# Hybrid encoder layer on one core: two gate projections moved behind the delta rule's first front, and attention's half of the output projection cut into 32 column-half units placed along the delta rule

## The chip, the cores and the metric

The kernel runs on one core of a Trainium2 chip. A core has five engines with their own instruction queues: TensorE (PE, matmuls, with PEld for the loads of its stationary operand), VectorE (DVE), ScalarE (ACT), GpSimd (POOL) and SyncE (SP), which here issues every DMA. Engines wait for each other through semaphores; each takes its instructions in the order in which they were written into its queue. The metric is the device time of one execution in microseconds (us).

## What is computed

One layer over a sequence of 2048 rows of 1024 features, in fp32:

```python
h = rms_norm(x, norm_w)
proj = h @ w_in
dn_q, dn_k, dn_v, dn_z, dn_beta, dn_decay, sw_q, sw_k, sw_v, sw_z = jnp.split(proj, cuts, axis=-1)
dn = gated_deltanet_bidir(dn_q, dn_k, dn_v, dn_beta, dn_decay, ...)   # 4 heads of 128, conv of 5, chunks, both directions
dn = rms_norm(dn, dn_out_norm_w) * silu(dn_z)
sw = windowed_gqa_with_sinks(sw_q, sw_k, sw_v, ...) * silu(sw_z)      # 8 query heads of 64, |i-j| <= 128
x = x + concatenate([dn, sw]) @ w_out
```

The delta rule solves a unit triangular system per chunk (the inverse of I + M), and then carries a 128 x 128 state through the chunks, forward and backward.

## The kernel before, in words

The sequence is 16 chunks of 128 rows, in two halves of eight. `phase_a` does the projections, the convolutions and attention; `phase_b` the delta rule and the output projection. Products that need more than one fp32r pass are split into a high and a low part, and three fp32r matmuls of 512 columns (hi x hi, hi x lo, lo x hi) add up in PSUM (L186 to L188, L558 to L560). Matmuls of the delta rule are plain fp32, which the profile records as two matmuls each.

For each half, `phase_a` projects keys, values and queries (L197 to L199), and then runs attention chunk by chunk (`attend`, L327 on: scores L339/L340, maximum L341, exponential L346, scaling L355, transposes L360, split L364/L365, product with the values L367/L368). Between chunks it writes "fillers" into the program: `gate_pairs` (tiles `pf_z`, 96 matmuls each: two pairs for attention's gates zsw, two for the delta rule's gates zdn) and `conv_pair` (tiles `pf_c`, 96 matmuls each, six pairs, with five VectorE taps at L237). `nfill` (L381) says how many fillers follow each chunk; in the second half it took six of ten, and the other four were written behind attention.

`phase_b` works head by head (0 to 3). `pre_front(h)` loads keys and queries (`kq`), transposes them (`tr`, L641), forms the Gram products (`gh`, L661), scales them with decays into the matrices `ma` (L670), writes the part to be inverted to DRAM (`m_d`) and scales the values (`trv`, L678). `pre_back(h)` reads `m_d` back into L, solves 32 x 32 blocks by 31 dependent pairs of VectorE operations (`tm`, L707, and `X`, L711), writes them to `x_d`, reads them in other layouts (`xc`) and completes the inverse with fp32 matmuls (`pi`, L735) and copies on GpSimd and ScalarE. `scan(h)` runs 16 steps in two directions: state times key (`pk`, L775), the residual `r` (L777), `py` (L784), `yk` (L789), the new state (L793, L796) and the outputs (L786, L802, `oacc`). `post` normalises them and writes `mix_dn`. A scan loads its keys and queries (`kqc`, L773) into four buffers per direction. In the program `pre_front(h + 1)` and `pre_back(h + 1)` follow `scan(h)`; the matrices of heads h and h + 2 share buffers (`hd[h % 2]`).

`out_sw` (L564) is attention's half of the output projection: it takes the attention results `mix_sw` chunk by chunk, splits them (`mhs` L550, `mls` L551), multiplies them with four row blocks of `w_out` (`wohs` L542, `wols` L543) into two PSUM tiles of 512 columns (`pcs`), adds the residual x (`xrs`, L561) and writes the sum to `part` in DRAM. It stands in the program between head 0's front and its solve, and its weights stay in SBUF for all 16 chunks. `out_dn` adds the delta rule's half (`pcd`) to `part` at the end. `warm` (L847) is 32, 32 and 20 matmuls of the identity with itself behind heads 1, 2 and 3; nothing reads them.

The order on each engine isn't that of the program. `set_order` (L892) takes all instructions with their dependences, the rings of buffers and the pools that share memory (a pool's users wait for those of the pool that held the space), gives each a price from `cost` and a delay from `LAG`, plans the five queues against each other, backward and forward, twelve times, and writes the order of the best plan into the program as fixed. It runs before the kernel is built; on the chip each engine follows that order.

Line numbers are those of the kernel before.

Of the kernel before, what the change touches and what calls it, by code (L numbers as in the profile page):

```python
# [7 lines left out]
F32 = mybir.dt.float32  # L8
F32R = mybir.dt.float32r
# [15 lines left out]
NDEC = 1  # L25
NEG = -1e30


def tile_hybrid(ctx, tc, t, out, dbg=None):
# [26 lines left out]
    with ExitStack() as ca:  # L56
        consts = phase_a(ca, tc, t, ident, nw, bd, gp, mix_sw, kq_d, v_d, zdn_d, zsw_d, dp)
    with ExitStack() as cb:
        phase_b(cb, tc, t, ident, consts, hp, mix_dn, mix_sw, kq_d, v_d, zdn_d, zsw_d, dp, out)
# [4 lines left out]
def phase_a(ctx, tc, t, ident, nw, bd, gp, mix_sw, kq_d, v_d, zdn_d, zsw_d, q_pool):  # L64
# [5 lines left out]
    with tc.using_default_side("right"):  # L70
        xp = ctx.enter_context(tc.tile_pool(reuse_waits="tile", name="xp", bufs=2))
        wp = ctx.enter_context(tc.tile_pool(reuse_waits="tile", name="wp", bufs=2))
        bp = ctx.enter_context(tc.tile_pool(reuse_waits="tile", name="bp", bufs=5))
        pj = ctx.enter_context(tc.tile_pool(reuse_waits="tile", name="pj", bufs=3, space=PSUM))
# [306 lines left out]
    nfill = ((2, 1, 1, 1, 1, 1, 1, 2), (2, 1, 1, 1, 1, 0, 0, 0))  # L381
# [40 lines left out]
    with tc.high_priority(-1000000):  # L422
        for f in fill:
            f()
    return consts
# [91 lines left out]
def phase_b(ctx, tc, t, ident, consts, hp, mix_dn, mix_sw, kq_d, v_d, zdn_d, zsw_d, dp, out):  # L517
# [57 lines left out]
    with tc.using_default_side("right"):  # L575
        hd = [pool("hd0"), None]
        q1 = pool("q1")
        ps_i = [pool("ps_i0", stack=pre_stack, space=PSUM)]
        ps_t = pool("ps_t", stack=pre_stack, space=PSUM)
        ps_g = pool("ps_g", stack=pre_stack, space=PSUM)  # L580
    rp = pool("rp", 2)
    qp = pool("qp", stack=pre_stack)
    ps_s = pool("ps_s", space=PSUM)
    ps_i.append(pool("ps_i1", stack=pre_stack, space=PSUM))
    XE = V
    zts = [[const(f"iv{j}_{i}", [P, 4, P], None, qp) for i in range(2 - j % 2)] for j in range(4)]
    for grp in zts:
        for a in grp:
            G.memset(a, 0.0)
# [10 lines left out]
    def kv_tile(kind, h, n, name):  # L600
        p, slot = ((0, n), (1, n), (2, n) if n < 2 else (0, n - 2), (0, 2 + n) if n < 2 else (1, n - 2))[h]
        return (hd[p] if p < 2 else qp).tile([P, 4, P], F32, tag=f"{kind}{slot}", name=name, bufs=1)

    def pre_front(h):
# [12 lines left out]
        for n, c4 in enumerate(FRONT):  # L617
# [71 lines left out]
    def pre_back(h, H):  # L689
        ma = H["ma"]  # L690
        m_d, x_d, mp = H["solve"]
        L0 = qp.tile([64, 32, 32], F32, tag="L0", name=f"L0{h}")
        L = qp.tile([P, 32, 32], F32, tag="L", name=f"L{h}")
        X = qp.tile([P, 32, 32], F32, tag="X", name=f"X{h}")
# [5 lines left out]
        G.memset(x, 0.0)  # L700
# [536 lines left out]
```

## Time and profile before

| | us |
|---|---|
| time, median of 3 runs | 1336.02 (1333.45 to 1339.87) |
| span of the profiled execution, first to last instruction | 1337.1 |
| PE / DVE / ACT / POOL busy in it | 1265.9 / 886.6 / 707.6 / 487.9 |
| mean granted TensorE clock | 0.988 |
| bytes moved by DMA | 199.10 MB, mean 149 GB/s |

The profile is of one execution; its span is the only time that it gives for that execution, and it lies within the spread of the runs. "Busy" is the time in which at least one instruction of the engine is recorded; records of successive matmuls overlap, so that a busy share near 100% doesn't yet mean that matmuls start as close as they can. The last column of a group of instructions is the idle time ahead of it and who ended it. A window row gives the busy time of each engine between two times, with the number of instructions in brackets.

### The profile page before, as it was taken

Reading aid. Unit: us, or ns where it says so; the run is one execution under the profiler, and the core shown is the slowest. Engines: PE = TensorE matmul, PEld = TensorE weight load, DVE = VectorE, ACT = ScalarE, POOL = GpSimd, SP = SyncE. Lnnn points to the kernel's source line nnn. Section 1 sums busy time; section 2 is a strip of 40 time slices with the busy share of each in tenths; the row PEclk is TensorE's granted clock in tenths of the full one; section 3 lists DMA queues with packets and bytes.
Section 4 is the critical chain, followed back from the end, with each engine's and each line's share of the span. In section 5 each row is a group of like instructions: output and inputs, shape, how many; then the busy total and the mean of one; then the engine's idle time right before and its main releaser. Section 6 shows DMA issues by size and latency. Waiting matters only on the chain.

```text
span 1337.1 us, 22922 instructions
## 1 busy us (share of the span) xinstructions
PE 1265.9 (95%) x7330; PEld 1083.1 (81%) x7330; DVE 886.6 (66%) x2250; ACT 707.6 (53%) x2105; POOL 487.9 (36%) x876
## 2 busy tenths in 40 slices
PE   5999999999999999999999899999979989898998
PEld 4998878888789988888888678778869878798776
DVE  4413387999856324778987898567884987846433
ACT  5422254766544333334766866229757867566310
POOL 1223033575602321002677654328238247070000
PEclk8999999999999999999999999999999999999999
DMA  7442344222552444323222767968476364333776
GB/s 243 129 139 82 115 142 133 98 88 93 177 178 88 134 146 135 114 71 105 87 94 93 264 198 228 279 197 214 121 193 171 97 198 117 97 107 107 230 239 216
DMA packets 219113, 199.10 MB, mean 149 GB/s; under 512 B 48240, under 2 KB 170736, under 8 KB 218992
## 3 DMA queue, kind: packets, MB, share of 16 engines
q1 hardware_dynamic: 218992, 197.63, 48.5%
q8 instruction: 59, 0.97, 0.3%
q14 instruction: 62, 0.51, 0.1%
HBM read 132.50 MB, written 65.08 MB: 148 GB/s over the span
## 4 chain that ended last, share of the span: by engine, by line
PE 67%; DVE 10%; DMA 9%; ACT 6%; POOL 3%; issue 2%; SPq 1%; DVEq 0%; POOLq 0%; ACTq 0%
PE pf_c L186 6%; PE pf_c L187 6%; PE pf_c L188 5%; PE pf_z L186 4%; PE pf_z L187 4%; PE pf_z L188 4%; PE pi L735 3%; PE pt L360 3%; PE pq_q L197 2%; PE pq_q L198 2%; PE pq_q L199 2%; PE pcd L559 2%; PE pcd L560 2%; PE pcd L558 2%; DMA xc<-x_d 2%
## 5 line engine op out<-in xcount | busy, mean ns | idle before, releaser
L237 DVE SCALAR_TENSOR_TENSOR acc<-pf_c,cw,acc 128x512 f32<-128x512 f32 (+1 forms) x192 | 140.1, 743 | 30.4 <-ACT acc L233 27.0
L186 PE MATMUL pf_c<-xhi,wh_c 128*128 128x512 f32 x384 | 148.7, 399 | 1.7 <-DVE acc L237 1.6
L187 PE MATMUL pf_c<-xlo,wh_c 128*128 128x512 f32 x384 | 148.5, 399 | 0.0
L188 PE MATMUL pf_c<-xhi,wl_c 128*128 128x512 f32 x384 | 147.7, 397 | 0.0
L355 POOL TENSOR_SCALAR pr<-pr,st 128x384 f32<-128x384 f32 (+1 forms) x128 | 84.4, 678 | 83.5 <-DVE st L353 59.1
L188 PE MATMUL pf_z<-xhi,wl_z 128*128 128x512 f32 x256 | 94.3, 400 | 0.0
L186 PE MATMUL pf_z<-xhi,wh_z 128*128 128x512 f32 x256 | 94.1, 399 | 0.0
L187 PE MATMUL pf_z<-xlo,wh_z 128*128 128x512 f32 x256 | 93.6, 397 | 0.0
L346 ACT ACTIVATE pr<-pr,st 128x384 f32<-128x384 f32 (+1 forms) x128 | 76.0, 596 | 27.1 <-DVE st L345 24.2
L186 PEld LDWEIGHTS pf_c<-xhi,wh_c 128*128 128x128 f32 x384 | 72.1, 188 | 17.6 <-DVE acc L237 2.2
L188 PEld LDWEIGHTS pf_c<-xhi,wl_c 128*128 128x128 f32 x384 | 72.1, 188 | 15.2
L187 PEld LDWEIGHTS pf_c<-xlo,wh_c 128*128 128x128 f32 x384 | 72.1, 188 | 14.3
L364 ACT ACTIVATE ph<-pt 128x512 fp32r<-128x512 f32 x92 | 53.7, 595 | 50.1 <-PE pt L360 42.4
L341 DVE CUSTOM_DVE_ANT_0 pr<-s,mask,sink 128x384 f32<-128x384 f32 (+1 forms) x128 | 72.9, 591 | 8.4 <-PE s L340 5.7
L360 PE MATMUL pt<-ident,pr 128*128 128x128 f32 x368 | 70.8, 276 | 2.5 <-POOL pr L355 2.1
L365 DVE TENSOR_TENSOR pl<-pt,ph 128x512 fp32r<-128x512 f32 x92 | 62.0, 683 | 12.7 <-ACT ph L364 11.6
L789 ACT ACTIVATE yk<-py,ck 128x128 f32<-128x128 f32 x120 | 44.1, 367 | 43.6 <-PE py L784 40.9
L360 PEld LDWEIGHTS pt<-ident,pr 128*128 128x128 f32 x368 | 47.8, 141 | 19.0 <-POOL pr L355 5.9
L670 DVE SCALAR_TENSOR_TENSOR ma<-gh,bp,dc 128x256 f32<-128x256 f32 x128 | 56.0, 475 | 10.2 <-PE gh L661 8.1
L233 ACT ACTIVATE acc<-pf_c,cw 128x512 f32<-128x512 f32 x48 | 32.6, 682 | 54.3 <-PE pf_c L188 48.8
L197 PE MATMUL pq_q<-wh_q,xhi 128*128 128x256 f32 x256 | 58.5, 284 | 0.2 <-ACT sgq L256 0.2
L561 DVE TENSOR_TENSOR xrd<-xrd,pcd 128x512 f32<-128x512 f32 x32 | 20.9, 683 | 55.8 <-PE pcd L560 48.0
(254 smaller groups left out, 3795.2 us busy)
## 6 DMA issues: line engine op xcount, KB each, us to landing
kqc<-kq_d SPq DMA_DIRECT2D x120, 128.0 KB, 2.6
ws_c<-wt SPq DMA_DIRECT2D x48, 256.0 KB, 3.6
xr<-x SPq DMA_DIRECT2D x16, 512.0 KB, 5.7
ws_z<-wt SPq DMA_DIRECT2D x32, 256.0 KB, 3.5
kq<-kq_d SPq DMA_DIRECT2D x16, 512.0 KB, 4.9
xrs<-x SPq DMA_DIRECT2D x32, 256.0 KB, 3.9
part<-xrs SPq DMA_DIRECT2D x32, 256.0 KB, 3.4
m_d<-ma SPq DMA_DIRECT2D x32, 256.0 KB, 4.8
```

Of the source, the lines that this page charges most:

```text
L186: T.matmul(ps, hi[:, k, cs], xhi[b][:, k], start=(k == 0), stop=False)
L187: T.matmul(ps, hi[:, k, cs], xlo[b][:, k], start=False, stop=False)
L188: T.matmul(ps, lo[:, k, cs], xhi[b][:, k], start=False, stop=(k == KC - 1))
L197: T.matmul(ps[:, :n], xh, hi[:, k, :n], start=(k == 0), stop=False)
L237: V.scalar_tensor_tensor(av, ps[:, lo:], cw[:, i, k : k + 1], av, ALU.mult, ALU.add)
L341: V.tensor_tensor_reduce(pr[j][:, :n], ps[:, :n], mask[:, lo * P : hi * P], 1.0, sink[:, hh : hh + 1], ALU.add, ALU.max, accum_out=mx[:, j ...
L346: A.activation(pr[j][:, :n], pr[j][:, :n], AF.Exp, bias=nm[:, j : j + 1], accum_out=den[:, j : j + 1])
L355: G.tensor_scalar(pr[j][:, :n], pr[j][:, :n], den[:, j : j + 1], 1.0, ALU.mult, ALU.mult)
L360: T.transpose(pt[:, j], pr[j][:, (kb - lo) * P : (kb - lo + 1) * P], ident)
L364: A.activation(ph, ptf, AF.Copy)
L365: V.tensor_tensor(pl, ptf, ph.bitcast(F32), ALU.subtract)
L670: V.scalar_tensor_tensor(ma[d, c4][:, c], gh[:, k], bp[:, d, cc : cc + 1], gms[d][:, c : c + 1].to_broadcast([P, 2, P]), ALU.mult, ALU.mult,)
```

## The change

- `nfill` of the second half becomes (2, 1, 1, 1, 1, 1, 1, 0): all six convolution pairs lie between chunks of attention. The remaining two fillers, the gate pairs of zdn, are handed to `phase_b` as `late` and written behind `pre_front(0)`. The pools that projections need (`xp`, `wp`, `bp`, `pj`) stay open until then, in a stack of their own (`wide`).
- `pre_back` is cut into `solve` (the 31 pairs) and `invert`. L0 is gone: the first half of L lands in X, is copied transposed out of it, and X is cleared afterwards. Pools are regrouped: `qa` for the solve, `qb` for the inversion.
- `out_sw` becomes `sw_units`: 32 units of one chunk and one half of the columns. A unit loads and splits its chunk itself, so that each chunk is loaded and split twice; the weights are loaded by halves of the columns into one set of buffers. Eight units are written ahead of `invert(0)`, one behind each group of the fronts of heads 2 and 3 (`FILLF`), and the last 16 behind `invert(3)`; PSUM is taken from tiles of the fronts and the inversion in turn.
- `warm` is gone.
- The planner's prices of five kinds of instruction change, and it gets more SBUF: the program's scratch for dynamic DMA shrinks from 16 KB to 1 KB per partition.

```diff
+N0 = 8
+FILLF = ((0, 0, 0, 0), (1, 1, 1, 1), (1, 1, 1, 1))
...
-    nfill = ((2, 1, 1, 1, 1, 1, 1, 2), (2, 1, 1, 1, 1, 0, 0, 0))
+    nfill = ((2, 1, 1, 1, 1, 1, 1, 2), (2, 1, 1, 1, 1, 1, 1, 0))
...
-    with tc.high_priority(-1000000):
-        for f in fill:
-            f()
-    return consts
+    return consts, fill
...
-    def out_sw(pool, bank, order):
-        w = load_wo(pool, 4, "s", "s")
-        for n, c in enumerate(order):
-            sc = slice(c * P, (c + 1) * P)
-            mx = pool.tile([P, 4, P], F32, tag="mx", name=f"mxs{c}", bufs=2)
+    def sw_units(pool):
+        w = {}
+
+        def weights(j):
+            wh = pool.tile([P, 4, 512], F32R, tag="wohs", name=f"wohs{j}", bufs=1)
+            wl = pool.tile([P, 4, 512], F32R, tag="wols", name=f"wols{j}", bufs=1)
+            for k in range(4):
+                st = pool.tile([P, 512], F32, tag="ws", name=f"woss{j}_{k}")
+                dma(st, t["wout"][:, 4 + k, j * 512 : (j + 1) * 512])
+                A.activation(wh[:, k], st, AF.Copy)
+                V.tensor_tensor(wl[:, k], st, wh[:, k].bitcast(F32), ALU.subtract)
+            w[j] = wh, wl
+
+        def unit(c, j, bank):
+            if j not in w:
+                weights(j)
+            wh, wl = w[j]
+            ns = slice(j * 512, (j + 1) * 512)
+            mx = pool.tile([P, 4, P], F32, tag="mx", name=f"mxs{c}_{j}", bufs=SWB[0])
             dma(mx, mix_sw[c])
-            out_half(pool, lambda j, nm: bank(n, j, nm), w, mx, t["x"][sc, :], part_d[c], f"s{c}", MB)
+            mh = pool.tile([P, 4, P], F32R, tag="mh", name=f"mhs{c}_{j}", bufs=SWB[1])
+            ml = pool.tile([P, 4, P], F32R, tag="ml", name=f"mls{c}_{j}", bufs=SWB[1])
+            A.activation(mh, mx, AF.Copy)
+            V.tensor_tensor(ml, mx, mh.bitcast(F32), ALU.subtract)
+            xr = pool.tile([P, 512], F32, tag="ws", name=f"xrs{c}_{j}")
+            dma(xr, t["x"][c * P : (c + 1) * P, ns])
+            ps = bank(f"pcs{c}_{j}")
+            for k in range(4):
+                T.matmul(ps, mh[:, k], wh[:, k], start=(k == 0), stop=False)
+                T.matmul(ps, ml[:, k], wh[:, k], start=False, stop=False)
+                T.matmul(ps, mh[:, k], wl[:, k], start=False, stop=(k == 3))
+            V.tensor_tensor(xr, xr, ps, ALU.add)
+            dma(part_d[c][:, ns], xr)
+
+        todo = [(c, j) for j in range(2) for c in range(NCH)]
...
+            if h:
+                for k in range(FILLF[h - 1][n]):
+                    fill(1, bank(k % 2))
...
-        dma(L0, lv[0])
+        dma(X[0:64], lv[0])
         dma(L[64:128], lv[1])
         x = X.rearrange("p r c -> p (r c)")
+        V.tensor_copy(L[0:64], X[0:64].rearrange("p r c -> p c r"))
         G.memset(x, 0.0)
         G.memset(x[:, ::33], 1.0)
-        V.tensor_copy(L[0:64], L0.rearrange("p r c -> p c r"))
...
-    def warm(h):
-        idle = ps_s.tile([P, P], F32, tag="pk", name=f"warm{h}")
-        for _ in range((32, 32, 20)[h]):
-            T.matmul(idle, ident, ident, start=True, stop=True)
+    def bank(k):
+        return lambda nm: (ps_t, ps_g, ps_i[0], ps_i[1])[k].tile([P, 512], F32, tag=("tr", "gh", "inv", "inv")[k], name=nm)
 
     H = pre_front(0)
+    for f in late:
+        f()
+    solve(0, H)
+    wide.close()
...
-    pre_back(0, H)
+    fill = sw_units(swp)
+    for n in range(N0):
+        fill(1, bank(2 + n % 2))
+    invert(0, H)
     for h in range(3):
         scan(h, H)
         H = pre_front(h + 1)
-        pre_back(h + 1, H)
-        warm(h)
+        solve(h + 1, H)
+        invert(h + 1, H)
+    for k in range(32):
+        fill(1, bank(k % 2))
...
             if "float32r" in str(i.ins[0].dtype):
-                return max(112, m / 2.4 + 14)
+                return max(112, 0.441 * m + 4)
...
-            return 60 + 0.86 * m + 85 * (scalars > 0) + 110 * (len(o) > 1)
+            short = len(o[0].ap) > 2 and o[0].ap[-1][1] <= 64
+            return 60 + 0.86 * m + 85 * (scalars > 0) + 110 * (len(o) > 1) + 100 * short
...
-        return 150 + 1.02 * m
+        return 190 + 1.02 * m
...
+        if eng[k] == "PE" and not insts[k][0].is_transpose and "float32r" not in str(insts[k][0].ins[0].dtype):
+            lag += 40
```

More of the change, by code (lines that the diff above doesn't have):

```diff
@@ L54, in tile_hybrid, with phase_a @@
     mix_dn = dp.tile([4, P, S], F32, tag="mix_dn", name="mix_dn")
[L56 to L59, printed above, removed]
+    with ExitStack() as cb, ExitStack() as wide:
+        with ExitStack() as ca:
+            consts, late = phase_a(ca, wide, tc, t, ident, nw, bd, gp, mix_sw, kq_d, v_d, zdn_d, zsw_d, dp)
+        phase_b(cb, wide, late, tc, t, ident, consts, hp, mix_dn, mix_sw, kq_d, v_d, zdn_d, zsw_d, dp, out)
     if dbg is not None:
         dbg(tc, locals())
[L64 removed]
+def phase_a(ctx, wide, tc, t, ident, nw, bd, gp, mix_sw, kq_d, v_d, zdn_d, zsw_d, q_pool):
     nc = tc.nc
@@ L514, in delta_setup, with phase_b @@
     return dmask, dnw, pw, beta, negc, ngc, egt, ekd, egc, gr_d, dec_d
-def phase_b(ctx, tc, t, ident, consts, hp, mix_dn, mix_sw, kq_d, v_d, zdn_d, zsw_d, dp, out):
+def phase_b(ctx, wide, late, tc, t, ident, consts, hp, mix_dn, mix_sw, kq_d, v_d, zdn_d, zsw_d, dp, out):
     nc = tc.nc
@@ L574, in phase_b @@
     pre_stack = ctx.enter_context(ExitStack())
[L575 to L589, printed above, removed]
+    hd = [pool("hd0")]
+    q1 = pool("q1", stack=pre_stack)
+    qa = pool("qa", stack=pre_stack)
+    ps_i = [pool("ps_i0", stack=pre_stack, space=PSUM), pool("ps_i1", stack=pre_stack, space=PSUM)]
+    ps_t = pool("ps_t", stack=pre_stack, space=PSUM)
+    ps_g = pool("ps_g", stack=pre_stack, space=PSUM)
     halves = slice(0, 64), slice(64, P)
```

63 lines of the change are left out of this document (36 added, 27 removed).

## The prediction

> **What bounds the kernel now.** I read the page first, then the table of windows (cut where the work changes its kind), then the count of single tiles in those windows, and last the chain and the order of time around the first triangular solve.
>
> ```profile
> span 1337.1 us, 22922 instructions
> PE 1265.9 (95%) x7330; PEld 1083.1 (81%) x7330; DVE 886.6 (66%) x2250; ACT 707.6 (53%) x2105; POOL 487.9 (36%) x876
> ```
>
> By the page TensorE is busy 95% of the span. A matmul's record is longer than its turn, though: records overlap. What counts is the spacing of starts.
>
> ```profile
> 520.00:560.00 40.00, 40.00 (x174) 32.53 (x174) 27.59 (x38) 12.00 (x19) 0.69 (x4) 1.00 0.33 102
> 994.37 1.73 PE L850 MATMUL warm<-ident 128*128 128x128 f32 x14
> L850 PE MATMUL warm<-ident 128*128 128x128 f32 x168 | 23.6, 284 | 0.0
> ```
>
> Between 520 and 560 us only 512-column projections run, without a gap: 40/174 = 0.230 us each. Fourteen records of a 128-column fp32 matmul (two records per matmul) take 1.73 us with the last one's 0.28: (1.73 - 0.28)/13 = 0.112 us each. A `gh` record has 256 columns, so I take twice that, 0.22. With these three spacings a window can be emptied of overlap.
>
> ```profile
> 463.00:600.00 137.00, 137.00 (x596) 111.38 (x595) 75.27 (x114) 48.51 (x97) 15.62 (x21) 1.00 0.40 119
> 600.00:745.00 145.00, 143.37 (x737) 116.75 (x735) 122.56 (x319) 98.72 (x248) 88.02 (x130) 1.00 0.34 109
> 745.00:843.00 98.00, 93.51 (x483) 74.92 (x483) 83.64 (x253) 70.55 (x220) 48.10 (x61) 0.98 0.70 221
> 843.00:885.00 42.00, 39.39 (x167) 31.63 (x166) 31.60 (x75) 6.56 (x15) 7.73 (x11) 0.96 0.89 281
> 885.00:1243.00 358.00, 320.14 (x2368) 292.01 (x2367) 255.25 (x829) 245.30 (x997) 163.49 (x379) 0.98 0.53 145
> 1243.00:1337.00 94.00, 89.38 (x393) 71.72 (x391) 32.90 (x56) 15.00 (x41) 1.64 (x1) 0.99 0.67 223
> ...
> 745.00:843.00 98.00, 52.17 (x185) 0.98 0.70 221
> 843.00:885.00 42.00, 38.96 (x163) 0.96 0.89 281
> 885.00:1243.00 358.00, 8.86 (x40) 0.98 0.53 145
> ...
> 885.00:1243.00 358.00, 25.65 (x92) 0.98 0.53 145
> ...
> 885.00:1243.00 358.00, 23.57 (x168) 0.98 0.53 145
> ```
>
> Columns: stretch, length, busy (count) of PE, PEld, DVE, ACT, POOL, clock, DMA share, GB/s. The second group is attention's output units (`pcs`), then come `gh` and `warm`, for PE alone. The stretches are: second half's gates and convolutions; attention with gates; attention with `pcs` and the first front; first solve under `pcs`; the delta rule of four heads; its output. The delta stretch holds 2368 records: 40 x 0.23 + 92 x 0.22 + 2236 x 0.112 = 280 us of issue in 358. So 78 us (22%) are stalls, and 168 x 0.112 = 18.8 us more are `warm`, which computes nothing. No other engine is near its limit there (DVE 255 of 358). That stretch is bound by chains: scan step, front, solve, inversion, scan. Ahead of it the engine is nearly full, and part of what fills it (348 `pcs` records between 745 and 885) has no deadline before the end.
>
> **The change part by part.** The built order of instructions says where things go; the prices are from rows.
>
> *Units out of the attention stretch.* In the new order no `pcs` matmul stands ahead of attention's end; 84 stand between the last `gh` of head 0 and the first inversion matmul, 300 after that. Head 0's front and the zdn gates stand behind attention; the gate work itself is unchanged in amount. So the work that now takes 463 to 843 us is the same but for 185 `pcs`: 380 - 185 x 0.23 = 337 us, which ends at 800. The filler's kind changes (convolutions now lie beside attention, gates beside front 0), so I keep the stalls of this stretch as they are. In the order 78 gate matmuls, 18 us, and 8 transposes stand behind front 0's last `gh`, so front 0 ends at about 780.
>
> *The first solve.* Its chain today (start, length), the copy from the order of time ahead of it:
>
> ```profile
> 851.60 1.10 DVE L702 COPY L<-L 64x1024 f32<-64x1024 f32 x1
> ...
> 840.59 6.57 DMA m_d<-ma
> 847.22 5.68 DMA L<-m_d
> ...
> 887.98 2.73 DMA x_d<-X
> ...
> 891.14 2.75 DMA xc<-x_d
> ...
> 896.20 1.17 PE pi L735 x8
> ```
>
> ```profile
> L670 DVE SCALAR_TENSOR_TENSOR ma<-gh,bp,dc 128x256 f32<-128x256 f32 x128 | 56.0, 475 | 10.2 <-PE gh L661 8.1 <-ACT dc L669 1.4
> L707 DVE TENSOR_TENSOR tm<-L,X 128x31 f32<-128x31 f32 (+15 forms) x124 | 47.8, 385 | 1.3 <-DMA L<-m_d 0.3
> L711 DVE TENSOR_TENSOR X<-X,tm 128x31 f32<-128x31 f32 (+15 forms) x124 | 44.6, 360 | 1.1
> L561 DVE TENSOR_TENSOR xrs<-xrs,pcs 128x512 f32<-128x512 f32 x32 | 21.8, 682 | 19.6 <-PE pcs L560 15.5 <-DMA xrs<-x 3.5 <-DMA xc<-x_d 0.4
> L551 DVE TENSOR_TENSOR mls<-mxs,mhs 128x512 fp32r<-128x512 f32 x16 | 11.0, 689 | 0.0
> L543 DVE TENSOR_TENSOR wols<-woss,wohs 128x512 fp32r<-128x512 f32 x8 | 5.8, 738 | 2.4 <-ACT wohs L542 2.3
> L550 ACT ACTIVATE mhs<-mxs 128x512 fp32r<-128x512 f32 x16 | 10.1, 632 | 40.8 <-PE pcs L560 34.3 <-DVE X L711 6.4
> L700 POOL MEMSET X<- 128x1024 f32 x4 | 3.8, 954 | 47.0 <-DMA x_d<-X 47.0
> L701 POOL MEMSET X<- 128x32 f32 x4 | 0.6, 159 | 0.1
> ```
>
> The 62 serial VectorE operations cost (47.8 + 44.6)/4 = 23.1 us. New between them, by the order, are 25 `ma` of front 1 (11.9), 4 `wols` (3.0), 3 gate products and 4 `xrs` at 0.68 (4.8), 5 `mls` (3.4) and 14 small ones (3, my estimate): together 49, and 48 with the few hundredths by which neighbours overlap. X now takes L0's place, so the memsets (0.95 + 0.16) wait for the copy out of it; on GpSimd the copies of the inversion wait behind them, and nothing else early. It is 1.1 us per solve, on the chain for head 0, taken as zero for the others, which have a scan to hide in (4.4 if not). Chain: 6.6 + 5.7 + 1.1 copy (today it ends before the other half of L lands; behind it now stand the memsets) + 1.1 + 48 + 2.7 + 2.75 + 2.3 to the first inversion matmul (891.14 + 2.75 to 896.20) = 70 us. First inversion at 780 + 70 = **850**, against 896. TensorE has in that time 84 `pcs` and 78 gates at 0.23, 68 transposes at 0.112 and 18 `gh` pairs at 0.44: 53 us. Some 17 us stall: the cover of this solve is thinner than the `pcs` of today.
>
> *Delta rule.* From the first inversion matmul to the output's first the new order has 320 inversion, 614 scan and 30 `gh` matmuls, 140 transposes and 300 `pcs`: 934 x 0.224 + 30 x 0.44 + 140 x 0.112 + 300 x 0.23 = **307 us**. `warm` is gone. What share stalls is the open number. From below it is nothing, as from 520 to 560; from above today's 22%. The nearest row is 843 to 885: units, with a serial solve beside them, 163 x 0.23 + 4 x 0.112 = 38 of 42 us, 10% stall. I take 10%: 307/0.9 = 341 us, ending at 850 + 341 = 1191.
>
> Head 1's front now ends ahead of scan 0. Today it runs in it, and that shows:
>
> ```profile
> 905.00:1000.00 95.00, 84.12 (x601) 75.48 (x600) 76.73 (x248) 69.05 (x307) 42.14 (x79) 0.98 0.69 180
> ...
> 1178.00:1241.00 63.00, 57.99 (x460) 54.54 (x460) 36.91 (x114) 43.52 (x153) 21.08 (x63) 1.00 0.38 113
> ```
>
> Scan 0, with front 1 and solve 1 beside it, takes 95 us; scan 3, with little but the rest of its inversion beside it, 63. Four scans of 63 are 252 us, well under 341. So chains leave room for the units if they are spread well.
>
> *What the units add.* Sixteen more splits: 16 x 0.632 = 10.1 us on ScalarE and 16 x 0.689 = 11.0 on VectorE, and 16 more 256 KB loads. They lie beside TensorE's work; VectorE would be at about 255 + 25 x 1.37 = 289 of 341, 85%. Uncovered they would cost 11. Each unit's store waits on SyncE for its sum, with the scan's `kqc` loads queued behind it:
>
> ```profile
> SPq L562 <- DVE xrs L561: 9.9, 8, 1.9
> ```
>
> The longest such wait was 1.9 us. A scan has four `kqc` buffers per direction, at 63/16 = 4 us a step some 12 us ahead, so I take zero; if each of 25 units cost its 1.9, 47. The smaller DMA scratch only gives room; zero, since the diff puts no transfer on another queue.
>
> *Clock.* The gate shows in today's trace around the first `warm`:
>
> ```profile
> 1000.00:1012.00 12.00, 0.00 (x0) 0.00 (x0) 0.00 (x0) 0.72 0.73 183
> ```
>
> The clock was 0.72 over 12 us, that is half speed for 6.7, a loss of at most 3.4 us, in spite of `warm`. The Trainium skill, "TensorE: Matmul & The Clock Gate", Part 1, says that an idle window of about 3.4 us halves the clock; that speaks against dropping `warm`. By that rule one window at each of three head boundaries costs 3 x 1.7 = 5 us and the sum would be 1290; I leave it out of the sum, as units stand at all three boundaries.
>
> *Output.* Unchanged, 94 us: 1191 + 94 = **1285**. The profiled span, 1337.1, is 1.1 above the median of the runs (1336.0), so **1284**.
>
> **Rivals.** (a) *The units stretch the chains* (slower). TensorE takes instructions in order: a unit in front of a scan step delays it, and if all steps are late already nothing is filled. Then the delta stretch is 347 (896 to 1243) less 11 for front 1 (48 transposes x 0.112, 28 `gh` records x 0.22) plus 300 x 0.23 = 405, and the time 850 + 405 + 94 = 1349. It decides from a stretch of 393, that is when a unit costs 2.3 of its 2.76 us. Against it: 78 us of stalls today, and scan 3's pace. (b) *Stalls keep their share*, 22%: 307/0.78 = 394, 1338, no change. For it: these stalls come from latencies that the fixed order did not foresee, and a new fixed order can miss them too. (c) *Stalls halve only to 15%*: 361, 1305; store waits of half their bound would do it. (d) *The fill is near perfect*, 3% by my estimate between those ends: 316, 1260. For it: projections run without gaps; against: the units come two 512-column buffers deep, weights for the second half of the columns are loaded into the same buffers midway. That the units stay where they were is excluded by the order.
>
> **How the numbers follow.** Forecast 1284 (1272 to 1296) 0.50; (c) 0.19; (d) 0.18; (b) 0.06; (a) 0.07. The range 1254 to 1322 leaves out (a), (b) and the low tail of (d), and takes in the bounds of the memsets and the splits. About 0.5% is what a measurement of this kernel can tell from no change: (a) is slower, (b) is the same, the rest faster: 0.87, 0.06, 0.07.
>
> **What would show it.** First inversion near 850 and no `pcs` before attention's end; PE stalls of some 17 us in the first solve; a delta stretch near 341 us with 307 of issue; scan 0 well under 95 us; no clock loss above 5 us. Wrong would be: scans of 90 us or more with units inside (a), SyncE waiting on `xrs` for over 20 us in sum with `kqc` late (c), or VectorE above 90% in the delta stretch, which would make it the bound.

## The result, and the profile after

The changed kernel takes **1303.86 us** (median of 4 runs, 1302.99 to 1304.68), the kernel before 1335.01 beside it: a ratio of 0.9752, 95% interval 0.9731 to 0.9773. That is 32 us gained of the 52 that the forecast of 1284 named. The page of the profiled execution of after:

```profile
span 1301.7 us, 22635 instructions
PE 1233.3 (95%) x7162; PEld 1057.1 (81%) x7162; DVE 895.6 (69%) x2266; ACT 719.8 (55%) x2121; POOL 501.8 (39%) x876
```

Its windows, cut where the work changes its kind (the columns of the windows in the prediction): second half's gates and convolutions, attention with convolutions, front 0 with the zdn gates, the first solve, the output:

```profile
463.00:600.00 137.00, 136.26 (x711) 114.08 (x710) 108.70 (x284) 92.69 (x240) 86.26 (x124) 1.00 0.41 125
600.00:737.00 137.00, 136.49 (x686) 111.73 (x685) 124.90 (x307) 87.04 (x200) 61.59 (x85) 1.00 0.31 96
737.00:793.00 56.00, 56.00 (x274) 46.20 (x272) 29.03 (x71) 28.85 (x115) 10.32 (x10) 1.00 0.71 212
793.00:862.00 69.00, 44.08 (x173) 31.15 (x172) 47.58 (x126) 33.60 (x140) 24.60 (x36) 0.88 0.86 258
...
1208.00:1301.00 93.00, 88.36 (x387) 70.49 (x385) 32.80 (x55) 15.67 (x41) 1.64 (x1) 1.00 0.67 232
```

The reader is to see one hole: TensorE is busy almost without a gap up to 793 us, and then 44 us of 69. The same trace cut at front 0's last `gh` (772.5), the first inversion matmul (862.2) and the output's first matmul (1205.0); the second pair of rows is `pcs` alone:

```profile
772.50:862.20 89.70, 64.58 (x268) 47.79 (x267) 55.17 (x143) 43.59 (x173) 29.91 (x43) 0.90 0.80 235
862.20:1205.00 342.80, 328.69 (x2367) 297.80 (x2368) 263.82 (x812) 235.54 (x892) 156.01 (x351) 0.99 0.61 178
...
772.50:862.20 89.70, 26.93 (x84) 17.10 (x84) 4.76 (x7) 0.90 0.80 235
862.20:1205.00 342.80, 110.90 (x300) 52.50 (x300) 17.10 (x25) 0.99 0.61 178
```

Before, the first inversion matmul stood at 896.2 and the output's first at 1241.4, 345.2 us apart, with no `pcs` between them:

```profile
896.20:1241.40 345.20, 309.80 (x2323) 283.94 (x2323) 248.60 (x809) 243.90 (x993) 160.66 (x371) 0.98 0.53 142
```

So **between these two traces the gain is the 34 us by which the first inversion comes earlier**. The stretch behind it is 2 us shorter and now holds 300 `pcs`, in the place of most of front 1 and of `warm`; the output is 1 us longer.

From the first solve to the first inversion of after: SyncE's queue in order of time, the landing of the solve's write (from issue, the last column), and TensorE.

```profile
843.12 0.32 SPq L740 DMA_DIRECT2D x_d<-X  x1
...
848.24 0.45 SPq L598 DMA_DIRECT2D part<-xrs  x1
848.78 0.44 SPq L658 DMA_DIRECT2D dc<-gr_d  x1
849.57 0.75 SPq L585 DMA_DIRECT2D mxs<-mix_sw  x1
850.37 0.57 SPq L751 DMA_DIRECT2D xc<-x_d  x1
```

```profile
x_d<-X SPq DMA_DIRECT2D x1, 512.0 KB, 3.5
```

```profile
856.65 0.79 PE L594 MATMUL pcs<-wohs,mhs 128*128 128x512 f32 x1 [4.27 <-ACT mhs L588]
...
862.22 1.13 PE L766 MATMUL pi<-iv,g 128*128 128x128 f32 x8 [0.87 <-DVE xrs L597]
```

The write is issued at 843.12 and lands 3.5 us later, but the first `xc` is issued only at 850.37: seven other issues stand between them in SyncE's queue, which accounts for the other 3.7 us (before, one did, and 2.7 us passed from 887.98 to 890.72). The inversion starts at 862.22, behind a unit that waited 4.27 us for its own split and load.

### The profile page after: what moved, and what is told of

It is laid out like the page before. It is cut to its first block, busy times and chain, and to the rows that moved or that the text cites. A ratio compares the mean times of both kernels' runs of the same rounds, so it can differ in the third digit from the quotient of the medians.

```text
span 1301.7 us, 22635 instructions
## 1 busy us (share of the span) xinstructions
PE 1233.3 (95%) x7162; PEld 1057.1 (81%) x7162; DVE 895.6 (69%) x2266; ACT 719.8 (55%) x2121; POOL 501.8 (39%) x876
## 4 chain that ended last, share of the span: by engine, by line
PE 73%; DVE 11%; DMA 6%; issue 3%; ACT 3%; POOL 3%; SPq 0%; DVEq 0%; POOLq 0%; ACTq 0%
PE pi L766 5%; PE pf_c L192 5%; PE pf_c L191 4%; PE pf_c L193 4%; PE pf_z L192 4%; PE pf_z L191 4%; PE pf_z L193 4%; DVE acc L242 3%; PE pt L365 2%; PE py L815 2%; PE po L824 2%; PE pcd L560 2%; PE pq_q L202 2%; PE pcd L562 2%; PE pcs L594 2%
## 5 line engine op out<-in xcount | busy, mean ns | idle before, releaser
L242 DVE SCALAR_TENSOR_TENSOR acc<-pf_c,cw,acc 128x512 f32<-128x512 f32 (+2 forms) x192 | 139.9, 742 | 15.0 <-ACT acc L238 12.9
L594 PE MATMUL pcs<-wohs,mhs 128*128 128x512 f32 x128 | 59.1, 462 | 10.9 <-ACT mhs L588 10.6
L595 PE MATMUL pcs<-wohs,mls 128*128 128x512 f32 x128 | 57.5, 449 | 0.5 <-DVE mls L589 0.3
```

Source lines behind the costliest of these rows:

```text
L242: V.scalar_tensor_tensor(av, ps[:, lo:], cw[:, i, k : k + 1], av, ALU.mult, ALU.add)
L594: T.matmul(ps, mh[:, k], wh[:, k], start=(k == 0), stop=False)
```

## Experiments

The theory after the result: the forecast failed in the first solve's chain, and what that chain loses is lost at the end. The rivals: what counts is how many matmuls stand in the delta stretch and what each costs there; or the planner and the memory, not the units, carry the gain. In each kernel below, the ratio is to the kernel before, with its 95% interval, and "stretch" is from the first inversion matmul to the output's first.

Two cautions hold for all of them. The kernel before took 1335.0 us beside the changed kernel and 1338.5 to 1340.2 beside the kernels below, so that the times below compare with 1303.9 only to some 5 us. And every edit has the five queues planned anew: the kernel in which only the planner's prices differ has the same work in the stretch as the changed kernel and takes 7.7 us more for it. A difference of that size in the stretch can't be put down to an edit alone.

**All units ahead of the first inversion.**

```diff
-N0 = 8
-FILLF = ((0, 0, 0, 0), (1, 1, 1, 1), (1, 1, 1, 1))
+N0 = 32
+FILLF = ((0, 0, 0, 0), (0, 0, 0, 0), (0, 0, 0, 0))
```

> All 32 units are written ahead of the first inversion; nothing else of the change is undone. In the built order 372 unit matmuls (of 384) then stand ahead of the first inversion matmul, against 84. Theory A (the delta rule is bound by chains, units are nearly free in its stalls): the first inversion comes some 60 us later, the delta stretch gets only 20 to 30 us shorter, time 1330 to 1345 us. Theory B (the delta stretch of the changed kernel is bound by TensorE, a unit costs there what it costs anywhere): within 8 us of 1304.

Measured: 1406.23 us, 1.0503 (1.0457 to 1.0549), above every number expected. The stretch falls to 304.8 us, but the first inversion comes at 1003.9. The `pcs` there, and what TensorE waited for in the same window of this kernel:

```profile
848.00:1004.00 156.00, 90.85 (x264) 59.72 (x264) 15.11 (x22) 0.85 0.66 196
```

```profile
PE pcs L594 <- ACT mhs L588: 19.6, 18, 2.4
PE pcs L595 <- DVE mls L589: 11.0, 18, 1.5
```

264 matmuls of 0.230 us are 61 us of issue; here TensorE is busy with them for 91 of the 156 us and waits 31 us for their splits. A unit has one buffer for its input, so that units behind one another wait for load and split. Neither theory held: so packed, a unit is dearer than either allowed.

**`warm` put back, and 24 of 32 units left out.** Two kernels that change the amount of work in the stretch, up and down.

```diff
         invert(h + 1, H)
+        idle = ps_s.tile([P, P], F32, tag="pk", name=f"warm{h}")
+        for _ in range((32, 32, 20)[h]):
+            T.matmul(idle, ident, ident, start=True, stop=True)
```

> The changed kernel with the 84 idle matmuls of warm put back (18.8 us of TensorE issue). Theory A: they go into stalls that are left, at most +6 us (1304 to 1310). Theory B: +15 to +19 us (1319 to 1323). If the clock gate took its toll where warm stood, the time would fall by up to 5 us.

```diff
...
-        todo = [(c, j) for j in range(2) for c in range(NCH)]
+        todo = [(c, j) for j in range(2) for c in range(NCH)][:8]
+        done.update(todo)
...
-        out_half(op, ..., part_d[c], ...)
+        out_half(op, ..., [(part_d[c] if (c, j) in done else t["x"][sc, :])[...] for j in range(2)], ...)
```

> Leaves out units 9 to 32 (three quarters of attention's half of the output; the residual x is added in their place), so that nearly no unit lies in the delta stretch: 288 matmuls, 66 us of issue, less. Theory A: the delta stretch shrinks from 346 us by 10 to 25 only, time 1278 to 1294. Theory B: by 55 to 66, time 1238 to 1249.

The second kernel's output lacks what these 24 units compute. Measured: with `warm` 1313.85 us, 0.9816 (0.9765 to 0.9867); with eight units 1269.75, 0.9485 (0.9444 to 0.9526). The stretch of the first, then that of the second:

```profile
861.70:1214.90 353.20, 343.60 (x2535) 316.43 (x2536) 261.93 (x812) 234.67 (x888) 156.15 (x353) 1.00 0.60 173
```

```profile
866.20:1172.20 306.00, 275.91 (x2061) 252.68 (x2059) 229.46 (x763) 216.27 (x843) 151.13 (x352) 0.97 0.50 140
```

The 168 matmuls of `warm`, 18.8 us of issue, lengthen the stretch by 10.4 us; 300 `pcs` fewer, 69 us, shorten it by 36.8. Both come to about **0.54 of the issue time**. With 8 us allowed either way for the new order, the 300 `pcs` give 0.42 to 0.65, so that neither "fills holes for nothing" nor "each costs all of it" held; the 10.4 us of `warm` alone are hardly more than what an order can make. What `warm` gains by the clock is at most some 3 us (1.00 against 0.99), less than it costs.

**The first eight units left out.**

```diff
-N0 = 8
+N0 = 0
...
-        todo = [(c, j) for j in range(2) for c in range(NCH)]
+        todo = [(c, j) for j in range(2) for c in range(NCH)][8:]
+        done.update(todo)
...
```

> Leaves out units 1 to 8 (the residual x is added in their place); the order has 24 unit matmuls ahead of the first inversion, against 84. Theory C (in the first solve the units' loads and VectorE's waits for their splits lengthen the chain, 89 us measured against 70 forecast): the first inversion comes 10 to 18 us earlier, time 1284 to 1296. Rival (front 1 alone lengthens it, and the units only fill a wait): first inversion within 4 us of 862, time 1295 to 1304, what is saved lying in the delta stretch.

Measured: 1300.99 us, 0.9712 (0.9668 to 0.9757): 22 us of issue removed for 3 us of time, 5 by the ratios. The first solve of this kernel and its stretch, then `pcs` alone:

```profile
772.40:858.20 85.80, 56.77 (x210) 41.37 (x208) 49.77 (x137) 46.06 (x194) 29.93 (x34) 0.72 0.76 207
...
772.40:858.20 85.80, 10.14 (x24) 7.21 (x24) 1.38 (x2) 0.72 0.76 207
858.20:1203.20 345.00, 96.92 (x264) 45.91 (x264) 15.06 (x22) 0.98 0.59 168
```

Units in the first solve are cheap: 60 matmuls fewer (13.8 us of issue) shorten it by 4 us. They are also not what makes it long: without most of them the solve still takes 53 us, and the clock falls to 0.72. The rival held by its two numbers, the first inversion at 858.2 and the time. But its reason, that the saving lies in the stretch, did not: there 36 `pcs` fewer (8.3 us) stand against 2 us more.

**Two decay buffers.** GpSimd masks front 1's decays (`dc`) beside the solve; the groups of VectorE within the first solve of after (786.5 to 843.2) are the reason to try:

```profile
L739 DVE TENSOR_TENSOR X<-X,tm 128x31 f32<-128x31 f32 (+15 forms) x31 | 14.8, 478 | 0.2
L697 DVE SCALAR_TENSOR_TENSOR ma<-gh,bp,dc 128x256 f32<-128x256 f32 x26 | 12.4, 476 | 2.6 <-PE gh L688 2.6
L735 DVE TENSOR_TENSOR tm<-L,X 128x31 f32<-128x31 f32 (+15 forms) x31 | 11.1, 358 | 1.5 <-POOL X L730 1.3
L589 DVE TENSOR_TENSOR mls<-mxs,mhs 128x512 fp32r<-128x512 f32 x5 | 3.4, 684 | 3.9 <-ACT mhs L588 3.9
L576 DVE TENSOR_TENSOR wols<-woss,wohs 128x512 fp32r<-128x512 f32 x4 | 2.7, 685 | 1.9 <-ACT wohs L575 1.9
L597 DVE TENSOR_TENSOR xrs<-xrs,pcs 128x512 f32<-128x512 f32 x4 | 2.7, 676 | 0.0
L215 DVE SCALAR_TENSOR_TENSOR zo<-zo,pf_z 128x512 f32<-128x512 f32 x3 | 2.1, 685 | 3.0 <-ACT zo L214 3.0
```

```diff
-NDEC = 1
+NDEC = 2
```

> The decays of head 1 are worked out beside head 0's, before attention of the second half, and read back: front 1 loses 8 GpSimd additions of the mask and 32 exponentials on ScalarE, which lay beside the first solve (8 of its subtractions took 1.1 to 1.5 us there in place of 0.3 to 0.4, while GpSimd added). Theory D (these additions lengthen the solve): the first solve takes 46 to 50 us in place of 56, first inversion 6 to 12 us earlier, time 1292 to 1300. Rival (VectorE's waits for other engines and the loads do it): solve above 53 us, time 1300 to 1308.

Measured: 1304.9 us, 0.975 (0.9727 to 0.9774). The same view of this kernel, 794 to 838.4:

```profile
L739 DVE TENSOR_TENSOR X<-X,tm 128x31 f32<-128x31 f32 (+15 forms) x31 | 11.4, 369 | 0.4
L735 DVE TENSOR_TENSOR tm<-L,X 128x31 f32<-128x31 f32 (+15 forms) x31 | 10.5, 338 | 0.5
...
L589 DVE TENSOR_TENSOR mls<-mxs,mhs 128x512 fp32r<-128x512 f32 x4 | 2.8, 690 | 0.8 <-ACT mhs L588 0.7
```

The solve is 12 us shorter (44.2 against 56.4), its stretched operations and the waits ahead of its splits are mostly gone. It begins 7 us later, its tail is 6 longer, and the first inversion stands at 863.2. The time is the same: theory D was right about the solve, the rival about the time.

**The planner's old prices.** The planner's four numbers as before, three in `cost` and one delay; nothing else.

```diff
-                return max(112, 0.441 * m + 4)
+                return max(112, m / 2.4 + 14)
...
-            return 60 + 0.86 * m + 85 * (scalars > 0) + 110 * (len(o) > 1) + 100 * short
+            return 60 + 0.86 * m + 85 * (scalars > 0) + 110 * (len(o) > 1)
...
-        return 190 + 1.02 * m
+        return 150 + 1.02 * m
...
-            lag += 40
+            lag += 0
```

> The planner's prices of before in the changed kernel (memory, units and the missing idle matmuls as in the changed kernel). If the gain comes from what the new layout of memory and the units allow: 1300 to 1312. If the corrected prices carry it (fewer stalls that the order did not foresee): 1314 to 1330.

Measured: 1310.96 us, 0.9792 (0.9771 to 0.9813). The stretch is 350.5 us, the first inversion at 864.0. The forecast for layout and units held, and the prices don't carry the gain. They are worth 7 us of the 32 by the times, 5 by the ratios, and the difference lies in the stretch (350.5 against 342.8).

**Front 1 behind solve 0.** The planner is told that head 1's loads, transposes and Gram products follow the last `X` of head 0.

```diff
+    solved = [k for x in used if x.startswith("X0_") for k in used[x]]
+    gate(solved, [k for x in used if x.startswith(("kq1_", "vt1_", "dc1_", "tr1_", "trv1_", "gh1_")) for k in used[x]])
```

> The planner is told that head 1's front follows head 0's solve; nothing else differs. Theory E (front 1's work in the queues lengthens the first solve, and is repaid in the delta stretch, which begins with a front already done): first inversion at 842 to 850 in place of 862, delta stretch 10 to 20 us longer, time 1298 to 1312. Rival (units and transfers lengthen the solve, front 1 does not): first inversion at 856 or later and the time at 1310 to 1325.

Measured: 1326.66 us, 0.992 (0.9894 to 0.9946). The solve takes 37.5 us, the shortest of all, and is followed by its longest tail. SyncE in this kernel, and its stretch:

```profile
823.68 0.32 SPq L740 DMA_DIRECT2D x_d<-X  x1
...
833.60 0.42 SPq L751 DMA_DIRECT2D xc<-x_d  x1
```

```profile
858.20:1231.30 373.10, 347.66 (x2417) 310.46 (x2417) 274.34 (x841) 252.03 (x963) 162.24 (x353) 0.97 0.63 182
```

The first inversion stands 4 us ahead of after's and the time is 23 us longer: front 1 now fills the tail and the stretch. Front 1 does lengthen the solve, as theory E had it, but the first inversion and the stretch (30 us longer) came out worse than its bounds, and the time above both forecasts.

**Front 0 in the projections' memory, as before.** The pools of the projections are closed ahead of the front, so that the front waits for them, and the last gate pairs are written in `phase_a` again.

```diff
-    return consts, fill
+    for f in fill:
+        f()
+    return consts, []
...
+    wide.close()
+    with tc.using_default_side("right"):
+        hd = [pool("hd0")]
...
-    wide.close()
+    rp = pool("rp", 2)
+    hd.append(pool("hd1"))
...
     with tc.using_default_side("right"):
-        rp = pool("rp", 2)
-        hd.append(pool("hd1"))
...
```

> Undoes the exchange of memory alone: the pools of the projections close before phase_b, and head 0's front takes their place, so that it waits for the gates and not for attention, as before the change; units, prices and the missing idle matmuls stay. Theory F (the exchange carries the gain: front 0 beside attention is slow): first inversion 15 to 34 us later than 862, time 1318 to 1338. Rival (units out of the attention stretch carry it, wherever front 0 stands): first inversion at 855 to 870, time 1296 to 1312.

Measured: 1325.85 us, 0.9915 (0.9893 to 0.9937). The gates are back beside attention (attention's last transposes start at 823 us instead of 724, the last gate matmuls at 743 instead of 791), front 0's last `gh` comes at 784.0, the first inversion at 875.2, and the stretch is 353.0. **Without the exchange of memory, which lets front 0 run before the gates are done, 22 of the 32 us are lost.** 13 of them show at the first inversion, 12 of these already at front 0's end, and 10 in the stretch, where 2.8 us are work that moved into it and the rest is no more than a new order can make. The time is in theory F's range, the first inversion 2 us short of it; the rival is out. Where the gates stand in the program has no part in it: the order built with `late` called inside `phase_a` is the same on every engine. These losses are not shares that add up: 22 here, 10 with `warm` put back and 7 with the old prices are more than the 32. No kernel here leaves the units beside attention with the rest of the change, so what moving them is worth by itself stays open.

**Units in front 1 instead of ahead of the first inversion.** Three kernels here, and one under the next heading, are for the tail of the first solve.

```diff
-N0 = 8
-FILLF = ((0, 0, 0, 0), (1, 1, 1, 1), (1, 1, 1, 1))
+N0 = 0
+FILLF = ((2, 2, 2, 2), (1, 1, 1, 1), (1, 1, 1, 1))
```

> The first eight units are no longer written in front of the first inversion into its own PSUM ring; two go behind each of front 1's four chunk groups and take the front's ring (tr, gh). All 32 units stay. After's tail (solve 0 ends 843.1, first pi 862.2) is 19.1 us. Theory G: TensorE runs in order, and units in the inversion's ring stand ahead of it, so pi waits for their loads (4.57 and 5.00 us idle) and for the add that empties the ring: without them the tail falls to 8 to 13 us (12.6 with the units left out), first pi at 850 to 857, the stretch to the output 340 to 346, time 1292 to 1300. Rival H: the tail is the trip of x_d and xc through DRAM under 258 GB/s and the planner merely packs other work there: first pi at 860 or later, time 1301 to 1308. If front 1, now with twelve units, gets long instead: stretch over 350, time 1305 to 1315.

Measured: 1304.99 us, 0.9754 (0.973 to 0.9779). The windows of this kernel, cut like those of after, and its SyncE:

```profile
770.80:849.60 78.80, 58.72 (x233) 42.54 (x232) 50.03 (x123) 32.85 (x123) 22.37 (x30) 0.83 0.69 202
849.60:1206.90 357.30, 339.86 (x2422) 305.57 (x2421) 268.13 (x832) 247.44 (x945) 160.44 (x364) 1.00 0.64 186
```

```profile
831.67 0.32 SPq L740 DMA_DIRECT2D x_d<-X  x1
838.61 0.50 SPq L751 DMA_DIRECT2D xc<-x_d  x1
```

**The first inversion comes at 849.6, where the forecast had it, and the time doesn't move.** The stretch grows by 14.5 us. Of these, 10 are work that moved into it (24 `pcs` x 0.23, 12 `gh` x 0.22, some 18 transposes x 0.112), the rest stalls. The first inversion came where theory G had it, but by a solve of 45.9 us, not by the tail: that is still 18.0 without units in the inversion's ring, and `xc` is issued 6.9 us behind `x_d`. Theory G falls for the time. The stretch is the long one of the third outcome, with the time at its lower edge (front 1 takes eight units here, not the twelve of the text); rival H had the time, but not the first inversion.

With eight units in front 2 as well:

```diff
-FILLF = ((2, 2, 2, 2), (1, 1, 1, 1), (1, 1, 1, 1))
+FILLF = ((2, 2, 2, 2), (2, 2, 2, 2), (1, 1, 1, 1))
```

> As the kernel with units in front 1 (eight there, none in the inversion's ring), and front 2 takes eight units where it took four; the output starts with 12 units left where it had 16. Tells whether units are cheaper inside a front than behind the last one. If the delta stretch is bound by chains, units cost the same 0.55 of their issue wherever they stand in it: stretch and time within 4 us of the units-in-front kernel. If the fronts have idle time that the last stretch lacks: 5 to 10 us faster than it. If a unit's single-buffered loads hold the in-order TensorE ahead of a scan, as in the packed kernel at some 5 us a unit: 8 to 20 us slower.

Measured: 1312.34 us, 0.9791 (0.9765 to 0.9817): slower by 7 than with units in front 1 alone, the first inversion at 849.3, the stretch 366.4. Of the three outcomes the dear one is nearest; that is no more than a new order can make, but nothing speaks for a front as a cheaper place for a unit.

With two decay buffers as well as units in front 1:

> Units in front 1 as above, with two decay buffers instead of one (alone that shortened the first solve from 56.4 to 44.2 us, the solve began 7 us later and the tail grew 6). If the tail's growth came from the units in the inversion's ring, both gains now add: first pi at 845 to 852, time 1284 to 1294. If the x_d and xc trip floors the tail, first pi 853 to 862 and time as the units-in-front kernel's within 4 us.

Measured: 1304.14 us, 0.9738 (0.9714 to 0.9763).

```profile
779.40:854.50 75.10, 56.41 (x223) 41.36 (x222) 48.23 (x123) 25.54 (x97) 13.39 (x26) 0.84 0.71 209
854.50:1207.70 353.20, 339.21 (x2421) 305.93 (x2419) 268.39 (x833) 244.51 (x938) 159.10 (x360) 1.00 0.65 188
```

The chain from front 0's last `gh` to the first inversion is 75 us, near the forecast's 70, but that `gh` comes 7 us later. The gains did not add, and the second outcome held by its numbers. Its cause did not: the first `xc` is issued 4.8 us behind `x_d` here, against 7.2 in after, and the tail still is 17.6 us.

**The unit's input two deep.**

```diff
-            mx = pool.tile([P, 4, P], F32, tag="mx", name=f"mxs{c}_{j}", bufs=SWB[0])
+            mx = pool.tile([P, 4, P], F32, tag="mx", name=f"mxs{c}_{j}", bufs=2)
-            ml = pool.tile([P, 4, P], F32R, tag="ml", name=f"mls{c}_{j}", bufs=SWB[1])
+            ml = mx.bitcast(F32R)
...
-                T.matmul(ps, ml[:, k], wh[:, k], start=False, stop=False)
-                T.matmul(ps, mh[:, k], wl[:, k], start=False, stop=(k == 3))
+                T.matmul(ps, mh[:, k], wl[:, k], start=False, stop=False)
+            for k in range(4):
+                T.matmul(ps, ml[:, k], wh[:, k], start=False, stop=(k == 3))
```

> The changed kernel with its units' input two deep at no more memory: the low part is written in place over the loaded tile (mx has two buffers, ml none of its own), and the four matmuls on the low part come last, so that mh is free 0.9 us earlier. The order packs 108 unit matmuls ahead of the first inversion where the changed kernel has 84. Theory I: what is lost between front 0's end and the first inversion is TensorE waiting for unit loads that can't be issued before the previous unit is done (4.57 and 5.00 us idle, 19.1 us of tail); with the next load under way the stalls shrink by 5 to 12 us, the first inversion comes at 860 to 868 with one unit more done, the stretch to the output falls to 330 to 338, time 1291 to 1298. Rival J: stalls are conserved (units in front 1 moved the first inversion 12.6 us ahead and the end by nothing), since the chain of front 1, solve 1 and scan 1 sets the later times: time 1301 to 1307. If unit writes over a buffer that a matmul still reads make DVE wait instead: 1308 to 1320.

Measured: 1315.07 us, 0.9815 (0.9794 to 0.9835). Its windows, and what TensorE waited for up to the first inversion, here (770 to 870) and in after (770 to 865):

```profile
774.50:864.40 89.90, 71.86 (x299) 53.15 (x297) 58.58 (x144) 44.93 (x176) 27.19 (x35) 0.91 0.79 234
864.40:1218.00 353.60, 331.70 (x2348) 299.09 (x2349) 263.16 (x812) 236.49 (x892) 155.96 (x357) 0.98 0.60 173
```

```profile
PE pcs L594 <- ACT mhs L588: 2.9, 2, 1.6
```

```profile
PE pcs L594 <- ACT mhs L588: 9.8, 2, 5.5
```

In its place theory I was right: 108 `pcs` instead of 84 fit into the same 90 us, and the wait for `mhs` fell from 9.8 to 2.9 us. The time is 11 us longer all the same. The stretch grew by 11 with 24 `pcs` fewer in it. Waits of VectorE on the shared buffer, the third outcome's cause, are not in its rows (2.7 us for `mxs` up to 870). Rival J forecast 1301 to 1307, so that stalls are not simply conserved either. The order of every engine was planned anew with this edit; which of its moves cost the stretch was not separated.

The stalls of these kernels, each window less its issue (counts by tile; 512 columns at 0.230 us, `gh` at 0.22, the rest at 0.112, as in the prediction):

| us | front 0's last `gh` | chain to first inversion, of it stalls | stretch, of it stalls | stalls in sum | time |
|---|---|---|---|---|---|
| forecast | 780 | 70, 17 | 341, 34 | 51 | 1284 |
| after | 772.5 | 89.7, 36 | 342.8, 36 | 72 | 1303.9 |
| units in front 1 | 770.8 | 78.8, 32 | 357.3, 40 | 72 | 1305.0 |
| the same, two decay buffers | 779.4 | 75.1, 30 | 353.2, 36 | 66 | 1304.1 |
| input two deep | 774.5 | 89.9, 30 | 353.6, 51 | 81 | 1315.1 |
| front 1 behind solve 0 | 772.0 | 86.2, 37 | 373.1, 58 | 95 | 1326.7 |

With the same matmuls to issue, the time can only follow the start, the sum of the stalls and the output behind it. Three edits shortened the first chain by 4 to 15 us; a later start and the stretch gave all or more of it back. Whether a chain of dependences hands the stalls on or each new order only brings its own, these kernels can't tell apart. None of the kernels with all the work beats the changed one by more than the noise.

## Why the prediction was right and wrong

**Direction and mechanism: right.** Units out of the attention stretch, front 0 ahead of the gates, the first inversion 34 us earlier (of the 46 forecast), `warm` not missed.

- *Front 0 at 780, gates at 800.* Measured 772.5 and 791: 8 us better. The stalls of that stretch, which the sum kept, shrank: by the windows TensorE was idle for 6.1 us between 463 and 843 before, and for 1.3 us between 463 and 793 after. That explains 5 of the 8.
- ***First-solve chain of 70 us: wrong, and the step that failed.*** It took 89.7, and the first inversion came at 862.2, not 850. Copy, memsets and the reads of `m_d` took 14.2 against 14.5 in the sum. The solve took 56.4 against 48: the count of new operations was nearly right (26 `ma`, 4 `wols`, 4 `xrs`, 5 `mls`), but they were summed as if none waited, and the group rows show some 13 us of idle time ahead of the operations there (`mls` 3.9 and `zo` 3.0 on ScalarE, `ma` 2.6 on TensorE). VectorE takes its queue in order, so the chain waited with them. It was busy for 43.8 us, 4 less than the sum, since neighbours overlap by more than the 1 us taken off; and that although `X` took 478 ns each where 360 were used. The tail took 19.1 against 7.75: 7.2 from `x_d` to the issue of `xc`, which the sum had at 2.73 by the landing alone, with nothing for SyncE's queue; 5.7 from there to the transpose of `xc` at 856.07, against 2.75; and 6.1 with a unit ahead of `pi`, against 2.3. SyncE's queue now holds front 1's and the units' loads ahead of `xc`; that queue was missing in the sum, and so was what these loads do to the transfers themselves. Between 852 and 862 the DMA engines are busy for the whole time, at 262 GB/s; before, the share was 0.60, at 191 GB/s, between 885 and 896. That the load made `xc` land later is argued from this; no kernel here changes it alone.
- ***17 us of stalls under it: mis-sized by the same step.*** 36. This is the hole from 793 to 862.
- *A delta stretch of 341 us with 307 of issue, 10% stalls: right in size*, 342.8 with 307 (300 x 0.23 + 60 x 0.22 + 140 x 0.112 + 1868 x 0.112). But the sum treated it as a length that follows the first inversion, and that is **not so**: where the first inversion came at 849.6, the stretch was 357. There, the forecast's 850 did not give the forecast's end. What the sum had to get right was the stalls of both windows together, 72 instead of 51. These 21 us and the miss of 20 are not quite the same thing: front 0's earlier end gave 7.5 back, and 6 came at the end. The output took 96.7 us from its first matmul where the sum had 94 (counted from 1243 instead of 1241.4, and 1 us longer), and the span now lies 2.2 us below the time where the sum took 1.1 off it.
- *Rival (a), 2.3 of 2.76 us per unit, and (b):* neither. A `pcs` in the stretch costs about 0.54 of its issue, 1.5 us per unit. The time came out where (c) stood, by another cause: the stretch has 10% stalls, not 15%. That it lies so far inside the range of 1254 to 1322 is in part luck: front 0's end, which the sum had 7.5 us too late, hid as much of the chain's error.
- *Scan 0 well under 95 us: right*, but the others did not fall to 63:

```profile
877.00:938.00 61.00, 59.13 (x464) 55.26 (x463) 55.32 (x178) 47.54 (x190) 31.14 (x62) 1.00 0.54 155
954.00:1031.00 77.00, 74.31 (x543) 67.49 (x541) 65.60 (x208) 63.00 (x257) 31.38 (x49) 1.00 0.67 193
```

- *Store waits on SyncE taken as zero: right.* In the whole span of after SyncE waits 7.4 us for `xrs`, seven times:

```profile
SPq L598 <- DVE xrs L597: 7.4, 7, 1.5
```

- *Memsets for heads 1 to 3 and splits at zero:* nothing measured speaks against it. VectorE is at 264 of 343 us (77%) in the stretch, under the 85 named.
- *No clock loss above 5 us: wrong for the first solve* (0.88 of 69 us, 8 us), where TensorE had little to do, *right for the stretch* (0.99 of 343, some 3 us):

```profile
852.00:862.00 10.00, 5.08 (x14) 3.16 (x12) 2.62 (x6) 1.03 (x2) 5.21 (x17) 0.83 1.00 262
1037.00:1044.00 7.00, 5.94 (x17) 4.14 (x17) 4.58 (x14) 3.57 (x11) 4.29 (x9) 0.53 0.69 171
```

The first row holds the idle window ahead of the unit at 856.65: 4.27 us without a matmul, and behind it the starts of `pcs` lie some 0.43 us apart instead of 0.23 until 859.7. The Trainium skill, "TensorE: Matmul & The Clock Gate", Part 1, has the clock halved by an idle window of about 3.4 us; the trace agrees there. Of the three head boundaries that the prediction priced by that rule, one shows a loss, 3.3 us (the second row). There no idle piece is longer than 1.8 us, but from 1033.9 to 1038.0, as the loss sets in, TensorE ran only one group of 1.1 us. Whether the lower clock lengthened the first solve was not separated.

## What to carry to other kernels

In a schedule where one engine is nearly full, add up issue and stalls of all stages to the end; a milestone reached earlier is no gain if the work that stood ahead of it moves behind it. When operations are put between the steps of a serial chain on an in-order engine, price each with the wait for its own inputs, not its duration alone. Here filler cost little in a stage that waits anyway (13.8 us of issue for 4 us in the first solve) and about half its length in one that is 90% full (69 us of issue for 37), as long as its buffers let it start; its loads stand in the same SyncE queue as the chain's own and have to be counted there. And where every edit brings a new order of all queues, find out first how far an order alone moves the time: here by some 8 us.

## What the hardware showed

VectorE's `X` operations, 0.36 us on average before (0.34 in the first solve, where GpSimd had nothing to do), took up to 1.5 us where GpSimd ran beside them. In after, VectorE first, then GpSimd:

```profile
814.48 1.50 DVE L739 TENSOR_TENSOR X<-X,tm 128x256 f32<-128x256 f32 x1
...
825.64 1.48 DVE L739 TENSOR_TENSOR X<-X,tm 128x231 f32<-128x231 f32 x1
```

```profile
813.92 1.78 POOL L659 TENSOR_TENSOR dc<-dc,dmask 128x512 f32<-128x512 f32 x1 [1.37 <-DMA dc<-gr_d]
...
825.20 1.67 POOL L659 TENSOR_TENSOR dc<-dc,dmask 128x512 f32<-128x512 f32 x1 [5.10 <-DMA dc<-gr_d]
```

GpSimd's operations end at 815.70 and 826.87, VectorE's at 815.98 and 827.12: in both cases 0.25 to 0.28 us behind. Both operations began while GpSimd's was running and ended only after it. The Trainium skill, "SBUF — State Buffer", section "Who interferes with whom", says that a VectorE instruction with two SBUF inputs contends with a GpSimd instruction that reads SBUF, and that one blocks the other for the whole instruction; the trace agrees, with these numbers. It cost the first solve some 3 us (31 x 0.11); the kernel with two decay buffers, where `X` took 369 ns, ended no earlier.

The trip of the solve's result through DRAM is made of queue as well as of transfer. `x_d` lands 3.5 us after its issue in after, 3.3 and 3.6 in the kernels with units in front 1 and with front 1 behind solve 0, but the first `xc` follows it by 7.2, 6.9 and 9.9 us. Where the queue added less, the landing took longer: 5.0, 5.6 and 6.5 us in the kernels without the first eight units, with the input two deep and with two decay buffers, and the first `xc` followed by 5.1, 7.3 and 7.0 us. So a shorter queue alone would not have brought `xc` forward to the 2.73 us of the sum.
